# Product and GELU of two 16 MB tensors: 32 KB load rows, and the first stores from the scalar engine's queue

## The chip, the cores and the metric

One core of a Trainium2 chip. The metric is device time in microseconds of one launch; the median of 3 runs of the kernel before is 120.79 us (120.77 to 120.79). Engines named below: DVE is the vector engine, ACT the scalar engine, SP the sync engine, which here only issues transfers. Transfers (DMAs) are carried by 16 DMA engines, whoever issues them.

## The reference

```python
batch, dim = 1024, 4096          # x and y, float32
z = x * y
out = 0.5 * z * (1 + np.tanh(np.sqrt(2 / np.pi) * (z + 0.044715 * z ** 3)))
```

That is the tanh form of GELU on an elementwise product. Two tensors of 16.8 MB are read and one is written: 50.33 MB in all.

## The kernel before

Each tensor is viewed as 128 partitions of 32768 float32 columns, where a partition's columns lie in one piece in memory. "Columns a to b" below always means these, on all 128 partitions; 8192 columns are 4 MiB.

`xs` holds all 32768 columns of x in SBUF. The product and the GELU are written over it in place, and the stores read from it. `ys` is a ring of 16384 columns for y.

Loads are issued by SP (lines 64 to 78): x in two pieces of 16384 columns (x0, x1), y in one piece of 16384 (y0) and two of 8192 (y1, y2), which take the ring's first and second half again. x0 and y0 are moved by `_hoist` ahead of the start-up barrier. y1 and y2 each wait until two, or four, products are done (line 77), since they overwrite what these read.

The arithmetic goes in eight steps of 4096 columns (`STEP`). For each, DVE multiplies `xs` by `ys` into `xs` (line 87) and raises `sem_mul`; ACT waits for that and applies the GELU in place (line 94) and raises `sem_act`. DVE waits for a piece of y and the matching piece of x only at the start of that piece of y (lines 84 and 85).

Stores are issued by SP too (lines 98 to 100), after all loads: columns 0 to 16384 after four GELUs, and 16384 to 32768 after eight. SP then waits for both stores, clears the range of semaphores and ends. All transfers thus stand in one queue, in the order x0, y0, x1, y1, y2, store 0, store 1, and each of a transfer's 128 rows is one piece of 64 KB or 32 KB, eight rows to a DMA engine.

Of the kernel before, what the change touches and what calls it, by code (L numbers as in the profile page):

```python
# [1 line left out]

# [4 lines left out]


F32 = mybir.dt.float32
GELU = mybir.ActivationFunctionType.Gelu_apprx_tanh  # L10


X_LOADS = [(0, 16384), (16384, 32768)]

Y_LOADS = [(0, 16384, 0), (16384, 24576, 0), (24576, 32768, 8192)]
STEP = 4096
STORES = [(0, 16384), (16384, 32768)]
Y_RING = 16384


def _hoist(nc, issued):

    here = nc.cur_bb.bb.instructions
    first = nc.main_func.blocks[0].instructions
    for ins in issued:
        del here[next(k for k, i in enumerate(here) if i is ins or i.name == ins.name)]
    engine = issued[0].engine
    at = next(
        k
        for k, i in enumerate(first)  # L30
        if i.engine == engine and type(i).__name__ == "InstDrain"
    )
    first[at:at] = issued


@with_exitstack
def kernel(
    ctx: ExitStack,
    tc: tile.TileContext,
    x: bass.AP,  # L40
    y: bass.AP,
    out: bass.AP,
):
    nc = tc.nc
    P = nc.NUM_PARTITIONS

    x_r = x.flatten_outer_dims().rearrange("(p a) c -> p (a c)", p=P)
    y_r = y.flatten_outer_dims().rearrange("(p a) c -> p (a c)", p=P)
    out_r = out.flatten_outer_dims().rearrange("(p a) c -> p (a c)", p=P)
    total_f = x_r.shape[1]  # L50


    tc.close()
    tc.compile()  # L54

    xs = nc.alloc_sbuf_tensor("xs", [P, total_f], F32).ap()
    ys = nc.alloc_sbuf_tensor("ys", [P, Y_RING], F32).ap()
    sem_x = [nc.alloc_semaphore(f"sem_x{i}") for i in range(len(X_LOADS))]
    sem_y = [nc.alloc_semaphore(f"sem_y{i}") for i in range(len(Y_LOADS))]
    sem_o = [nc.alloc_semaphore(f"sem_o{i}") for i in range(len(STORES))]  # L60
    sem_mul = nc.alloc_semaphore("sem_mul")
    sem_act = nc.alloc_semaphore("sem_act")

    def load_x(i):
        a, b = X_LOADS[i]
        return nc.sync.dma_start(out=xs[:, a:b], in_=x_r[:, a:b]).then_inc(sem_x[i], 16)  # L66

    def load_y(i):
        a, b, r = Y_LOADS[i]
        return nc.sync.dma_start(  # L70
            out=ys[:, r : r + b - a], in_=y_r[:, a:b]
        ).then_inc(sem_y[i], 16)

    _hoist(nc, [load_x(0).ins, load_y(0).ins])
    load_x(1)
    for i in (1, 2):
        nc.sync.wait_ge(sem_mul, (Y_LOADS[i][1] - Y_LOADS[1][0]) // STEP)
        load_y(i)

    n = 0  # L80
    for i, (a, b, r) in enumerate(Y_LOADS):
        for j, (xa, xb) in enumerate(X_LOADS):
            if xa <= a < xb:
                nc.vector.wait_ge(sem_x[j], 16)
        nc.vector.wait_ge(sem_y[i], 16)  # L85
        for c in range(a, b, STEP):
            nc.vector.tensor_mul(  # L87
                out=xs[:, c : c + STEP],
                in0=xs[:, c : c + STEP],
                in1=ys[:, r + c - a : r + c - a + STEP],  # L90
            ).then_inc(sem_mul, 1)
            n += 1
            nc.scalar.wait_ge(sem_mul, n)
            nc.scalar.activation(  # L94
                out=xs[:, c : c + STEP], in_=xs[:, c : c + STEP], func=GELU
            ).then_inc(sem_act, 1)

    for i, (a, b) in enumerate(STORES):
        nc.sync.wait_ge(sem_act, b // STEP)
        nc.sync.dma_start(out=out_r[:, a:b], in_=xs[:, a:b]).then_inc(sem_o[i], 16)  # L100
    for i in range(len(STORES)):
        nc.sync.wait_ge(sem_o[i], 16)
    nums = sorted(s.num for s in [*sem_x, *sem_y, *sem_o, sem_mul, sem_act])
    assert nums == list(range(nums[0], nums[-1] + 1))
    nc.sync.sem_clear(range(nums[0], nums[-1] + 1))


# [1 line left out]
_INS = ['x', 'y']  # L109
_OUTS = [((1024, 4096), 'float32')]  # L110


# [23 lines left out]
```

## Time and profile before

| | us |
|---|---|
| median of the runs | 120.79 |
| the profiled execution | 120.85 |
| its span, first to last instruction | 119.5 |
| one product, DVE, 128 x 4096 (8 of them) | 4.42 |
| one GELU, ACT, 128 x 4096 (8 of them) | 3.62 |
| SP's issue of one DMA | 0.33 to 0.43 |
| SP waiting for products before y1 and y2 | 56.2 |
| SP waiting for GELUs before the stores | 33.8 |

The page gives each engine's busy time, a strip of 40 slices of the span with a digit for the busy share in each, and the queues' share of the 16 DMA engines' time. The chain lists what ended last, followed back to what released it. For DMAs the trace gives the time of issue on the queue of the engine that issues ("SPq") and the time from issue to landing, which includes waiting behind earlier transfers in the queue. L87 means line 87 of the kernel before.

### The profile page before, as it was taken

Reading aid. Unit: us, or ns where it says so; the run is one execution under the profiler, and the core shown is the slowest. Engines: PE = TensorE matmul, PEld = TensorE weight load, DVE = VectorE, ACT = ScalarE, POOL = GpSimd, SP = SyncE. Lnnn points to the kernel's source line nnn. Section 1 sums busy time; section 2 is a strip of 40 time slices with the busy share of each in tenths; the row PEclk is TensorE's granted clock in tenths of the full one; section 3 lists DMA queues with packets and bytes.
Section 4 is the critical chain, followed back from the end, with each engine's and each line's share of the span. In section 5 each row is a group of like instructions: output and inputs, shape, how many; then the busy total and the mean of one; then the engine's idle time right before and its main releaser. Section 6 shows DMA issues by size and latency. Waiting matters only on the chain.

```text
span 119.5 us, 68 instructions
## 1 busy us (share of the span) xinstructions
DVE 35.0 (29%) x8; ACT 30.2 (25%) x9; POOL 0.2 (0%) x4
## 2 busy tenths in 40 slices
DVE  0000000000000199999600049959990000000000
ACT  3000000000000006797780000977479200000000
POOL 0000000000000000000000000000000000000000
DMA  9889888998899889988898989998899888988890
GB/s 351 351 373 680 351 351 351 636 417 351 351 636 417 351 351 526 526 351 351 351 526 351 504 373 482 395 526 351 351 395 658 351 351 351 702 351 351 351 680 22
DMA packets 1008, 50.33 MB, mean 421 GB/s; under 512 B 112, under 2 KB 112, under 8 KB 112
## 3 DMA queue, kind: packets, MB, share of 16 engines
q1 hardware_dynamic: 1008, 50.33, 98.5%
HBM read 33.55 MB, written 16.78 MB: 421 GB/s over the span
## 4 chain that ended last, share of the span: by engine, by line
DMA 53%; DVE 22%; ACT 3%; SPq 0%; issue 0%; DVEq 0%
DMA ys<-in_y_dram 53%; DVE xs L87 22%; ACT xs L94 3%; SPq L66 0%; DVEq L85 0%
## 5 line engine op out<-in xcount | busy, mean ns | idle before, releaser
L87 DVE TENSOR_TENSOR xs<-xs,ys 128x4096 f32<-128x4096 f32 x8 | 35.0, 4421 | 54.7 <-DMA ys<-in_y_dram 54.7
L94 ACT ACTIVATE xs<-xs 128x4096 f32<-128x4096 f32 x8 | 28.9, 3617 | 61.1 <-DVE xs L87 61.1
L94 ACT ACT_TABLE_LOAD x1 | 1.3, 1283 | 1.9 <-PEq L54 1.9
L120 POOL MEMSET const-bfloat16-1.0<- 128x1 bf16 x1 | 0.1, 102 | 0.0
L120 POOL MEMSET const-uint8-127<- 128x1 uint8 x1 | 0.1, 102 | 0.0
L120 POOL MEMSET const-float32-1.0<- 128x1 f32 x1 | 0.1, 99 | 0.0
L120 POOL MEMSET const-float32-0.0<- 128x1 f32 x1 | 0.1, 98 | 0.2 <-issue 0.2
## 6 DMA issues: line engine op xcount, KB each, us to landing
ys<-in_y_dram SPq DMA_DIRECT2D x2, 4096.0 KB, 21.1
xs<-in_x_dram SPq DMA_DIRECT2D x2, 40.3
out_dram<-xs SPq DMA_DIRECT2D x2, 31.9
ys<-in_y_dram SPq DMA_DIRECT2D x1, 40.8
```

Source lines behind the costliest of these rows:

```text
L87: nc.vector.tensor_mul(out=xs[:, c : c + STEP], in0=xs[:, c : c + STEP], in1=ys[:, r + c - a : r + c - a + STEP],).then_inc(sem_mul, 1)
L94: nc.scalar.activation(out=xs[:, c : c + STEP], in_=xs[:, c : c + STEP], func=GELU).then_inc(sem_act, 1)
L120: nc = _bacc.Bacc("TRN2", target_bir_lowering=False, num_devices=1)
```

## The change

X and y are both loaded in four pieces of 8192 columns. SP's order of issue becomes x0, y0 (hoisted), x1, y1, x2, x3, then y2 after two products and y3 after four. Output is stored in four pieces: columns 0 to 4096 and 4096 to 8192 are issued by ACT, each right after the GELU that finishes it; 8192 to 24576 (after six GELUs) and 24576 to 32768 (after eight) are issued by SP behind the loads. Stores of 4096 columns have rows of 16 KB. SP no longer waits for the last store before it clears the semaphores: that store's semaphore is left out of the cleared range, waited for last, and lowered by 16 in the same instruction.

```diff
-X_LOADS = [(0, 16384), (16384, 32768)]
+X_LOADS = [(0, 8192), (8192, 16384), (16384, 24576), (24576, 32768)]
-Y_LOADS = [(0, 16384, 0), (16384, 24576, 0), (24576, 32768, 8192)]
+Y_LOADS = [(0, 8192, 0), (8192, 16384, 8192), (16384, 24576, 0), (24576, 32768, 8192)]
 STEP = 4096
-STORES = [(0, 16384), (16384, 32768)]
+STORES = [(0, 4096), (4096, 8192), (8192, 24576), (24576, 32768)]
+EARLY = 2
...
+    def store(engine, i):
+        a, b = STORES[i]
+        engine.wait_ge(sem_act, b // STEP)
+        engine.dma_start(out=out_r[:, a:b], in_=xs[:, a:b]).then_inc(sem_o[i], 16)
+
     _hoist(nc, [load_x(0).ins, load_y(0).ins])
     load_x(1)
-    for i in (1, 2):
-        nc.sync.wait_ge(sem_mul, (Y_LOADS[i][1] - Y_LOADS[1][0]) // STEP)
+    load_y(1)
+    load_x(2)
+    load_x(3)
+    for i in (2, 3):
+        nc.sync.wait_ge(sem_mul, (Y_LOADS[i][1] - Y_RING) // STEP)
         load_y(i)
...
             ).then_inc(sem_act, 1)
+            if n <= EARLY:
+                store(nc.scalar, n - 1)
 
-    for i, (a, b) in enumerate(STORES):
-        nc.sync.wait_ge(sem_act, b // STEP)
-        nc.sync.dma_start(out=out_r[:, a:b], in_=xs[:, a:b]).then_inc(sem_o[i], 16)
-    for i in range(len(STORES)):
+    for i in range(EARLY, len(STORES)):
+        store(nc.sync, i)
+    for i in range(len(STORES) - 1):
         nc.sync.wait_ge(sem_o[i], 16)
-    nums = sorted(s.num for s in [*sem_x, *sem_y, *sem_o, sem_mul, sem_act])
+    nums = sorted(s.num for s in [*sem_x, *sem_y, *sem_o[:-1], sem_mul, sem_act])
...
     nc.sync.sem_clear(range(nums[0], nums[-1] + 1))
+    nc.sync.wait_ge(sem_o[-1], 16).then_inc(sem_o[-1], -16)
```

More of the change, by code (lines that the diff above doesn't have):

```diff
@@ L59 @@
     sem_y = [nc.alloc_semaphore(f"sem_y{i}") for i in range(len(Y_LOADS))]
-    sem_o = [nc.alloc_semaphore(f"sem_o{i}") for i in range(len(STORES))]
     sem_mul = nc.alloc_semaphore("sem_mul")
     sem_act = nc.alloc_semaphore("sem_act")
+    sem_o = [nc.alloc_semaphore(f"sem_o{i}") for i in range(len(STORES))]
     def load_x(i):
```

## The prediction, made before the changed kernel was run

> **What bounds the kernel now.** I read the slices of the page first, then the DMA queue, the chain, the DMA issues with their times to landing, and last the start in narrow windows.
>
> ```profile
> span 119.5 us, 68 instructions
> DVE 35.0 (29%) x8; ACT 30.2 (25%) x9; POOL 0.2 (0%) x4
> ...
> DMA  9889888998899889988898989998899888988890
> ...
> q1 hardware_dynamic: 1008, 50.33, 98.5%
> ```
>
> The vector engine works 35 of 119.5 us and the scalar engine 30; the 16 DMA engines work all the time, on one queue. So the end is set by bytes divided by the rate, plus any moment in which the ring of transfers runs dry. There is none now. The chain in order of time shows what the arithmetic hides under:
>
> ```profile
> 0.44 40.80 DMA ys<-in_y_dram
> ...
> 41.34 17.43 DVE L87 TENSOR_TENSOR xs<-xs,ys 128x4096 f32<-128x4096 f32 x4 [41.34 <-DMA ys<-in_y_dram]
> 45.80 3.62 ACT L94 ACTIVATE xs<-xs 128x4096 f32<-128x4096 f32 x1 [42.59 <-DVE xs L87]
> ...
> 62.45 31.22 SPq L100 DMA_DIRECT2D out_dram<-xs  x2
> 70.47 8.76 DVE L87 TENSOR_TENSOR xs<-xs,ys 128x4096 f32<-128x4096 f32 x2 [11.70 <-DMA ys<-in_y_dram]
> ...
> 80.88 8.76 DVE L87 TENSOR_TENSOR xs<-xs,ys 128x4096 f32<-128x4096 f32 x2 [1.66 <-DMA ys<-in_y_dram]
> ```
>
> The first line is from the chain (start, length), the others from the timeline. The first store is issued at 62.45, when the loads still need until 80.8: it waits in the ring, and the rings go from loads to stores without a pause. The first store carries 19.3 us of work, and the second is issued at 93.3, before the first has ended. That order is what hides the last products and GELUs.
>
> Issue plus time to landing gives the landings. The spread of each line's issues is:
>
> ```profile
> L66 SPq DMA_DIRECT2D xs<-in_x_dram x2: 328/357/386, 0.0 to 1.9; - x2
> DMA to landing us min/median/max: 21.9/40.3/58.7
> ...
> L70 SPq DMA_DIRECT2D ys<-in_y_dram x3: 328/328/433, 0.4 to 58.8; - x3
> ...
> DMA to landing us min/median/max: 20.2/22.0/40.8
> ...
> L100 SPq DMA_DIRECT2D out_dram<-xs x2: 343/346/348, 62.4 to 93.3; - x2
> ...
> DMA to landing us min/median/max: 26.1/31.9/37.7
> ```
>
> Landings: y0 0.44+40.8 = 41.24; x1 1.93+58.7 = 60.6; y1 50.13+20.2 = 70.3; y2 58.80+22.0 = 80.8; store 0 62.4+37.7 = 100.1; store 1 93.3+26.1 = 119.4. Call 8192 columns (4 MiB) a unit. Differences: x1 19.4 for two units, y1 9.7 for one, y2 10.45 for one, store 1 19.3 for two. So a unit takes 9.67 us, loaded or stored, in 64 KB or in 32 KB rows, with one exception: the load just before the first store took about 0.75 more. The start costs 41.24 - 4 x 9.67 = 2.56. Of it 1.0 is from the issue to the first row:
>
> ```profile
> 0.00:1.00 1.00, 0.00 (x0) 0.00 (x0) 0.20 (x4) 1.00 0.00 0
> 1.00:2.00 1.00, 0.00 (x0) 0.07 (x1) 0.00 (x0) 1.00 3.13 1049
> ```
>
> (The last two columns are DMA share and GB/s, booked at the start of a row.) The other 1.56 is filling the pipeline and the receipt at the end.
>
> **What the Trainium skill says.** All from "DMA: Bandwidth & Descriptors". *Where 436 GB/s comes from*: a ceiling of 435.2 GB/s. The trace agrees: store 1, 8.39 MB in 19.3 us, is 435 GB/s; there is no faster rate to win while engines move one row at a time. *Queues, rings and completion order*: each DMA engine takes turns between queue rows that have work, a packet at a time. The kernel before has one queue, so nothing in its trace shows this. *Anatomy of one DMA*: DMA engines don't wait on semaphores; the issuing sequencer does, before dispatch. The trace agrees: store 0 was issued at 62.45, right after the fourth GELU (58.80+3.62). So a store whose GELU is late is not in the ring at all.
>
> **The change, part by part.** Times on the profiled execution's axis.
>
> *All loads in 32 KB rows.* The skill (same page, *Why small descriptors are slow*) prices a packet at about 3 cycles, 3.5 ns at its 850 MHz. Rows per engine go from 56 to 96 (eight for each of 7 transfers before; of 12 after), so 40 x 3.5 ns = 0.14 us as an estimate; the two row sizes measured above can't be told apart. I take 0.15. What moves is the first arithmetic: y0 with 8192 columns lands at 2.56 + 2 x 9.67 = 21.9 and not at 41.24. The vector engine starts at 22.0; two products (8.77) end at 30.8. SP issues four loads at 1.9 without waits, then y2 (waits for product 2, 30.8) and y3 (product 4). Ring order on SP: x0 y0 x1 y1 x2 x3 y2 y3, then the two late stores.
>
> *Early stores from the ACT queue.* GELU 1 runs 26.5 to 30.1 and ACT issues store 0 (about 0.35, from the SP issues). GELU 2 can start only at 30.8, when product 2 ends, so the issue and its wait on ACT's own GELU are covered; without that cover they would shift ACT by 0.35, which nobody awaits there. GELU 2 ends at 34.4, store 1 follows. From 31.1 on, each engine has 16 rows of 16 KB on the second ring, each 9.67/16 = 0.60 us. In turn with 32 KB load rows (1.21) they are through after 16 turns of 1.81, at about 60. They are bytes that had to be moved anyway, only earlier: the sum of bytes is unchanged. y1 lands at 2.56 + 38.7 + 4.8 = 46.1, product 4 ends at 54.9, y3 is issued then; x2, x3 and y2 lie before it in the ring until 80, so that wait is covered by 25 us.
>
> *What a change between load and store rows costs* is the unknown, 16 times. From above: the 0.75 before the first store now, 16 x 0.75 = 12 us. From below: nothing, if two rings are fetched ahead separately; and less than nothing if a store row and a load row overlap in an engine, at most all 9.67 us. I take 0.03 each, 0.5 in all, because 0.75 appears once per stage and looks like a refill that a second ring already has in hand.
>
> *The late stores.* Here is the cost that decides. Loads and early stores together are nine units: y2 (the eighth unit in effect) lands at 2.56 + 8 x 9.67 + 0.1 = 80.0, y3 at 89.7. After y3 the rings are empty unless a late store has been issued. Store 2 covers columns 8192 to 24576 and so waits for GELU 6, which needs y2: start 80.1, two products 8.77, to 88.9; GELU 3.62, to 92.5. First row 1.0 later, 93.5. So the DMA engines stand idle from 89.7 (89.3 without the receipt) to 93.5, about 4 us, where before they never did. Then the pipeline fills again: between 0.3 and 1.2 (load start above: 1.56 less a receipt of about 0.35); I take 0.8. Then three units, 29.0, and the receipt 0.35: 93.5 + 0.8 + 29.0 + 0.35 = 123.7. Store 3 must be ready before store 2 is through at 113: y3's products run 89.8 to 98.5, GELU 8 to 102.2. It is, with 11 us to spare. The 0.75 before the first store goes away in the gap; it isn't in this sum.
>
> *Short end.* The range clear is done before the last wait. From the last landing, 119.4, to the end of the span, 119.5, is 0.1: the gain is 0 to 0.1, I take 0.05.
>
> Sum: 123.7 + 0.1 - 0.05 = 123.75 without the cost of changes, 124.25 with it. Against the span of 119.5 that is +4.7. Outside the span the profiled execution had 120.85 - 119.5 = 1.35; it lies 0.06 above the median of 120.79, so the forecast is 120.79 + 4.7 = 125.5.
>
> **Rivals.**
> *Dear changes (slower still).* Each change of direction costs more than 0.2 us, up to the 0.75 seen. For it: y2's 10.45 against 9.7. Against it: seen once, in one ring. Everything after 31 moves later by 16 times the price, the gap stays: 125.0 + 3.2 to 12 = 128.2 to 137.
> *Overlap (faster).* In the mixed stretch of 31 to 60 us a store row's read of SBUF and write of HBM run beside a load row's opposite directions in the same engine. Price: up to 9.67 saved, which would give 125.0 - 9.67 = 115.3. It decides once more than 4.2 us, 43% of the early stores, is hidden. For it: load and store share neither side of the path. Against it: stages of pure loads and pure stores run at the same 435 GB/s, which speaks for a limit inside the engine that both share. Less than 43% gives 121 to 124.5.
> *The stores don't take turns.* If ACT's rows get through only when SP's ring is empty, they move at 79.9 to 89.6, fill the gap, and y2 lands 9.67 earlier; store 2 is then ready at 83. Nothing is idle, and the 0.75 stays: 120.79 + 0.15 - 0.05 = 120.9.
>
> **How the numbers follow.** My own case (changes at most 0.2 each, fill 0.3 to 1.2) gives 124.3 to 128.2: chance 0.60. Dear changes 0.17, about half of it under 131. Overlap past the threshold 0.13, below it 0.05. No turns 0.05. The range reaches from 120.6 (no turns) to 131, leaving out the overlap and the dear half of the changes, about 0.2. A measurement here tells 0.2% (0.24 us) from no change. Faster 0.14 (overlap, and a part of no turns); same 0.03 (no turns); slower 0.83.
>
> **What would show it.** Right: a second DMA queue moving from about 31 to 60; DMA share of zero between about 90 and 93.5, and the chain running y2, two products, GELU 6, store 2 to the end; SP waiting for ACT at line 78. The rate in 31 to 60 gives the price of a change: 435 GB/s is none, 400 about 0.15 each. Wrong: y2 landing well before 80 (overlap), the ACT queue moving after 70 (no turns), or no idle stretch after y3.

## The result, and the profile after

The changed kernel takes 125.1 us (median of 6 runs, 124.97 to 125.42), the kernel before in the same comparison 120.87. The ratio is 1.0348, 95% interval 1.0327 to 1.0369: slower by 3.5%. The forecast was 125.5. The profiled execution took 124.97, its span is 123.6.

The arithmetic is what it was; the page of the changed kernel shows the difference in the strip of the DMA engines (slices of 3.1 us) and in a second queue:

```profile
span 123.6 us, 75 instructions
...
DMA  9897989999979989989999997979707997793977
GB/s 329 350 509 339 509 371 477 392 456 466 376 307 466 498 350 424 498 355 429 429 488 445 403 509 339 509 339 509 339 0 339 572 445 339 339 678 170 509 339 339
...
q1 hardware_dynamic: 1440, 46.14, 87.6%
q10 hardware_dynamic: 288, 4.19, 7.9%
```

One slice moves nothing, the thirtieth: 89.6 to 92.7. Before, the one queue was busy for 98.5% of the span; now the two are for 95.5%. Narrow windows give the edges (as in the prediction, the last two columns are DMA share and GB/s):

```profile
88.00:89.00 1.00, 1.00 (x1) 0.75 (x1) 0.00 (x0) 1.00 1.21 524
89.00:90.00 1.00, 0.43 (x1) 0.54 (x1) 0.00 (x0) 1.00 0.01 0
90.00:91.00 1.00, 0.63 (x1) 1.00 (x1) 0.00 (x0) 1.00 0.00 0
91.00:92.00 1.00, 1.00 (x1) 1.00 (x1) 0.00 (x0) 1.00 0.00 0
92.00:93.00 1.00, 1.00 (x1) 1.00 (x1) 0.00 (x0) 1.00 0.00 0
93.00:94.00 1.00, 1.00 (x1) 0.08 (x1) 0.00 (x0) 1.00 1.07 459
```

A row's bytes are booked where it starts, so the stretch from 89 to 90, which shows nothing, still holds the ends of rows. By the records of single rows (the trace has the start, length, size and queue of each) the last row of y3 ends at 89.89 and the first row of store 2 starts at 93.95: 4.06 us idle. The timeline of the changed kernel (start, length, engine, line) names what they waited for:

```profile
80.67 8.76 DVE L96 TENSOR_TENSOR xs<-xs,ys 128x4096 f32<-128x4096 f32 x2 [25.95 <-DMA ys<-in_y_dram]
85.13 3.62 ACT L103 ACTIVATE xs<-xs 128x4096 f32<-128x4096 f32 x1 [26.76 <-DVE xs L96]
89.46 3.62 ACT L103 ACTIVATE xs<-xs 128x4096 f32<-128x4096 f32 x1 [0.72 <-DVE xs L96]
90.37 8.76 DVE L96 TENSOR_TENSOR xs<-xs,ys 128x4096 f32<-128x4096 f32 x2 [0.94 <-DMA ys<-in_y_dram]
93.11 10.05 SPq L78 DMA_DIRECT2D out_dram<-xs  x2
```

y2's products start at 80.67, GELU 6 ends at 93.08, SP issues store 2 at 93.11. The chain of waits doesn't show this: it follows the instruction that ended last, GELU 8 at 102.8, back through y3, and is silent on the transfers after it. No store is on it; SP's own waits do have the late one:

```profile
DMA ys<-in_y_dram 64%; DVE xs L96 14%; ACT xs L103 3%; SPq L67 0%; DVEq L94 0%
...
SPq L78 <- ACT xs L103: 47.4, 2, 38.0
```

Where DMA is the bound, as here, the windows find a hole and the timeline explains it.

### The profile page after: what moved, and what is told of

It is laid out like the page before. It is cut to its first block, busy times and chain, and to the rows that moved or that the text cites. A ratio compares the mean times of both kernels' runs of the same rounds, so it can differ in the third digit from the quotient of the medians.

```text
span 123.6 us, 75 instructions
## 1 busy us (share of the span) xinstructions
DVE 35.0 (28%) x8; ACT 30.2 (24%) x9; POOL 0.2 (0%) x4
## 4 chain that ended last, share of the span: by engine, by line
DMA 64%; DVE 14%; ACT 3%; SPq 0%; issue 0%; DVEq 0%
DMA ys<-in_y_dram 64%; DVE xs L96 14%; ACT xs L103 3%; SPq L67 0%; DVEq L94 0%
```

## The experiments

All edits are on the changed kernel unless said otherwise. Medians in us, ratios to the kernel before in the same comparison.

| run | median | ratio, 95% interval |
|---|---|---|
| e1_split_late_store | 120.81 | 0.9993 (0.9986 to 1.0) |
| e2_no_early_stores | 120.83 | 0.9993 (0.9983 to 1.0003) |
| e3_loads_alone | 120.96 | 1.0 (0.9991 to 1.001) |
| e4_early_8KB_rows | 124.46 | 1.0293 (1.028 to 1.0306) |
| e5_early_4KB_rows | 120.56 | 0.9967 (0.9955 to 0.9978) |
| e6_tiny_store_at_start | 120.96 | 1.0003 (0.9995 to 1.0011) |
| e7_tiny_store_at_30us | 120.89 | 0.9995 (0.9986 to 1.0004) |
| e8_late_wait_alone | 124.5 | 1.0297 (1.0282 to 1.0311) |
| e9_4KB_and_split | 120.95 | 1.0003 (0.9996 to 1.001) |
| e10_2KB_and_split | 122.61 | 1.0144 (1.0129 to 1.016) |
| e11_4KB_again | 120.57 | 0.9974 (0.9966 to 0.9981) |

The theory: a late store waits for a GELU that comes after the rings have run dry (the gap theory). The main rival: loads and stores in turn slow each other (the mixing theory).

**Take the wait away, keep the mixing.**

```diff
-STORES = [(0, 4096), (4096, 8192), (8192, 24576), (24576, 32768)]
+STORES = [(0, 4096), (4096, 8192), (8192, 16384), (16384, 24576), (24576, 32768)]
```

> Edit: the late store of columns 8192 to 24576 becomes two, 8192 to 16384 (needs GELU 4) and 16384 to 24576 (needs GELU 6). Gap theory: GELU 4 ends at about 58, so the first of them is in the ring long before y3 lands at 90, moves until about 99.5, and GELU 6 is done at 93; no idle stretch, about 4.1 us less than the changed kernel: 121.0, or 120.3 if the once-paid 0.7 us at the first store next to loads isn't paid again when loads go over to stores. Rival (mixing loads and stores is what costs): the mixed stretch is unchanged, so the time stays near 125.

Timeline of this kernel:

```profile
58.36 35.14 SPq L78 DMA_DIRECT2D out_dram<-xs  x2
80.72 8.76 DVE L96 TENSOR_TENSOR xs<-xs,ys 128x4096 f32<-128x4096 f32 x2 [26.04 <-DMA ys<-in_y_dram]
```

The first late store is issued at 58.36; y2's products start at 80.72, against 80.67 in the changed kernel. The mixed stretch is the same to 0.05 us, the rows leave no idle stretch once they have begun, and 120.81 is 4.3 below the changed kernel. All of the loss is gone.

**Take the mixing away, keep the wait.**

```diff
-STORES = [(0, 4096), (4096, 8192), (8192, 24576), (24576, 32768)]
-EARLY = 2
+STORES = [(0, 24576), (24576, 32768)]
+EARLY = 0
```

> Edit: no early store at all; two stores behind the loads, columns 0 to 24576 (needs GELU 6) and 24576 to 32768. Gap theory: y3 lands at about 80, GELU 6 ends at 82.9, first store row 83.7; idle about 4.0; then four units of 9.67: span 122.9 to 123.2, time 124.2 to 124.5 (the once-paid 0.7 falls into the gap). Mixing theory: nothing is mixed, so 120.8.

Windows and timeline of this kernel:

```profile
80.00:81.00 1.00, 0.79 (x1) 1.00 (x1) 0.00 (x0) 1.00 0.00 0
81.00:82.00 1.00, 1.00 (x1) 1.00 (x1) 0.00 (x0) 1.00 0.00 0
82.00:83.00 1.00, 1.00 (x1) 0.90 (x1) 0.00 (x0) 1.00 0.00 0
83.00:84.00 1.00, 1.00 (x1) 0.00 (x0) 0.00 (x0) 1.00 1.85 786
```

```profile
79.28 3.62 ACT L103 ACTIVATE xs<-xs 128x4096 f32<-128x4096 f32 x1 [0.72 <-DVE xs L96]
80.21 8.76 DVE L96 TENSOR_TENSOR xs<-xs,ys 128x4096 f32<-128x4096 f32 x2 [0.96 <-DMA ys<-in_y_dram]
82.93 10.07 SPq L78 DMA_DIRECT2D out_dram<-xs  x2
```

No store is early, nothing is mixed, and the same hole is there, ten microseconds sooner (rows 79.71 to 83.85: 4.14 us). The time is 124.5. With the two runs together the gap is the cause and the mixing isn't.

**The other parts of the change.** e2 has the change's loads and its short end, but two stores of 16384 columns behind the loads; e3 also has the old end.

```diff
-STORES = [(0, 4096), (4096, 8192), (8192, 24576), (24576, 32768)]
-EARLY = 2
+STORES = [(0, 16384), (16384, 32768)]
+EARLY = 0
```

> Edit: EARLY = 0 and the stores of the kernel before (two of 16384 columns, behind the loads, from SP); load rows and short end as changed. Gap theory: first store needs GELU 4 only, nothing idle; 120.6 to 120.9, as before. Mixing theory: the same. Theory that the load rows or the order x2, x3 ahead of y2 cost: above 121.5.

> Edit: only the 32 KB load rows and their order; stores and end as in the kernel before. The profile shows y0 and x0 in 0.2 us less than half of the time before, against 32 more rows per engine less 0 for stores at about 4 ns: 120.6 to 120.9. Less e2_no_early_stores, this is what the short end is worth: 0 to 0.1 us.

Both equal the kernel before within their intervals. (Two readings in the expectation of e3 are off: x0 and y0, landing at 21.7 where it was 41.2, took more than half of the time before, and the 0.2 us holds only against the predicted 21.9; and an engine has 24 more load rows, not 32.) The short end, 120.96 - 120.83 = 0.13, isn't resolved by intervals of 0.1% on each side.

**Are changes of direction free?** Smaller early rows mean more of them.

```diff
-STORES = [(0, 4096), (4096, 8192), (8192, 24576), (24576, 32768)]
-EARLY = 2
+STORES = [(0, 2048), (2048, 4096), (4096, 6144), (6144, 8192), (8192, 24576), (24576, 32768)]
+EARLY = 4
...
-        engine.wait_ge(sem_act, b // STEP)
+        engine.wait_ge(sem_act, -(-b // STEP))
```

(A store whose last column lies inside a step now waits for that step's GELU. Not shown: the loop in which ACT, after each GELU, issues all early stores that this GELU finishes. Runs e5 and e9 to e11 have both edits too, e7 the wait.)

> Edit: the early stores in four pieces of 2048 columns (rows of 8 KB), so 32 store rows per engine among the loads and not 16; the late stores as in the changed kernel. Gap theory with free changes of direction: 16 more rows at 4 ns, 125.1 to 125.4. If each change of direction costs 0.05 us (the 0.8 us missing in the mixed stretch, spread over 16 rows): 16 more of them, 125.9. If the 0.8 is paid once at the first store: no more than 125.4.

124.46: twice the changes of direction took 0.6 less, which neither theory had in its numbers. The trace shows why it fits the gap theory. The last row of y3 ends at the same time (89.88, against 89.89). But the 32 small store rows of each engine, one after each load row, reach to about 81, past the landing of y2, so fewer store bytes are moved ahead of y2. Its products start at 80.26 (80.67), store 2 is issued at 92.70 (93.11), and the hole is shorter by 0.4. So with 4 KB rows the hole should nearly close:

```diff
-STORES = [(0, 4096), (4096, 8192), (8192, 24576), (24576, 32768)]
-EARLY = 2
+STORES = [(k, k + 1024) for k in range(0, 8192, 1024)] + [(8192, 24576), (24576, 32768)]
+EARLY = 8
```

> Edit: early stores in eight pieces of 1024 columns (rows of 4 KB), late stores as in the changed kernel. Gap theory: y3 and the early stores still end at 89.9, but in turn with 40 load rows only 40 of the 64 store rows come before the end of y2; 24 rows of 0.15 us fewer stand before it, so y2 lands near 77.1, GELU 6 ends near 89.6, first late row 90.5: idle 0.6 instead of 4.1, total 121.3 to 121.9. Theory that the time is lost by mixing, or per change of direction: 48 changes more than the changed kernel has, so 125 or later.

The timeline and the windows of this kernel:

```profile
75.50 8.76 DVE L96 TENSOR_TENSOR xs<-xs,ys 128x4096 f32<-128x4096 f32 x2 [24.20 <-DMA ys<-in_y_dram]
...
86.43 8.76 DVE L96 TENSOR_TENSOR xs<-xs,ys 128x4096 f32<-128x4096 f32 x2 [2.17 <-DMA ys<-in_y_dram]
87.94 11.27 SPq L78 DMA_DIRECT2D out_dram<-xs  x2
```

```profile
86.00:87.00 1.00, 0.57 (x1) 1.00 (x1) 0.00 (x0) 1.00 1.04 426
87.00:88.00 1.00, 1.00 (x1) 0.92 (x1) 0.00 (x0) 1.00 1.02 418
88.00:89.00 1.00, 1.00 (x1) 0.00 (x0) 0.00 (x0) 1.00 1.03 422
```

y2's products start 5.2 us sooner than in the changed kernel (3.6 expected), y3 has landed by 86.4, and the early rows left over are moved alone at nearly the full rate until store 2 arrives. No hole, 120.56. The theory by change of direction (125 or later) falls. The 1.6 us by which y2 came sooner than expected are about what a miscount makes: the expectation put 40 store rows of each engine ahead of y2, and the records have 29 before y2's last row starts. The expectation let the early rows take turns with x1 too, but x1 lands at 31.6 and the first early row of most engines starts near 35. Eleven rows of 0.15 us are 1.65.

**Does 4 KB beat the kernel before, and does the split add to it?** e9 splits e5's late store at 16384; e10 does so with 2 KB rows; e11 is e5 once more.

```diff
-STORES = [(k, k + 1024) for k in range(0, 8192, 1024)] + [(8192, 24576), (24576, 32768)]
+STORES = [(k, k + 1024) for k in range(0, 8192, 1024)] + [(8192, 16384), (16384, 24576), (24576, 32768)]
```

> Edit: early stores in rows of 4 KB as in e5_early_4KB_rows, and the late store split at 16384 as in e1_split_late_store. e5 had no idle stretch left, so the gap theory gives the split nothing more: 120.4 to 120.7, the same as e5 within its spread. If e5's lead over the kernel before (0.33%) comes from small rows where loads and stores first meet (the 0.7 us cost less there), it stays; if it was scatter of few runs, 120.8 to 120.95.

> Edit: as e9_4KB_and_split with early rows of 2 KB (16 pieces of 512 columns). If smaller rows make the first meeting of loads and stores cheaper still: 0.2 to 0.4 below e9, about 120.2. If what small rows save is used up at 4 KB, or the 64 rows more at about 4 ns each (0.26 us) and 8 more issues on ACT count: 120.6 to 121.

> The kernel of e5_early_4KB_rows once more, in five rounds, because e9_4KB_and_split didn't keep its lead and its profiled execution shows transfers ending no earlier than before (119.04 against 119.07). If the lead is real, 120.5 to 120.6 against 120.9; if it was the scatter of eight runs on one chip, within 0.1% of the kernel before.

e11 repeats e5 (ratio 0.9974, 0.9966 to 0.9981): a gain of 0.26%, small but clear of no change, and the fastest form found. e9 loses it. The longest time to landing of an early store shows a difference:

```profile
DMA to landing us min/median/max: 15.5/42.1/82.7
```

That is e9; e5 has 15.1/41.4/53.4. With a late store already in SP's ring, the early rows never get the engines to themselves and go on in turn until the end, 36.9 + 82.7 = 119.6. Where exactly the 0.4 us are lost there is not shown. e10 fails in another way. Timeline of this kernel:

```profile
37.55 45.91 ACTq L78 DMA_DIRECT2D out_dram<-xs  x8
...
83.51 10.63 ACT L103 ACTIVATE xs<-xs 128x4096 f32<-128x4096 f32 x3 [45.99 <-issue]
```

The first eight issues on ACT took 0.37 to 0.50 us each; of the second eight, the first took 0.34, the next 11.2, and the last was not over before 83.5. ACT stood in its own issues for 46 us. GELU 3, whose product was done at 46.3, started at 83.51, and the first late store was issued at 90.66. The early rows left over kept the engines busy until 90.39; from there to 91.51 nothing moves, so 1.1 us of hole are back. The rest of the 2.0 us by which e10 is above e11 wasn't taken apart, nor what held ACT.

**The 0.7 us of the first store.** The prediction saw 0.75 us lost just before the first store of the kernel before. The two probes start from e2.

```diff
+    nc.vector.memset(warm, 0.0).then_inc(sem_w[0], 1)
+    nc.scalar.wait_ge(sem_w[0], 1)
+    nc.scalar.dma_start(out=out_r[:, 0:128], in_=warm).then_inc(sem_w[1], 16)
...
+    nc.sync.wait_ge(sem_w[1], 16)
     for i in range(EARLY, len(STORES)):
         store(nc.sync, i)
```

> Edit on the kernel without early stores: a small tile is filled by the vector engine and 128 columns of it (rows of 512 B) are stored from ACT at about 2 us, over columns that the proper store writes again later. Question: the 0.7 us which the first store costs the loads beside it. If it is a once-paid cost of the first store while the fill at the start hides it: gone at 80, total 120.1. If it is once paid but not hidden: y0 lands 0.7 later, total 120.8. If it belongs to going over from loads to stores in one queue: still there at 80, total 120.8 to 120.9 with y0 not later.

For e7:

```diff
-STORES = [(0, 16384), (16384, 32768)]
-EARLY = 0
+STORES = [(0, 128), (128, 16384), (16384, 32768)]
+EARLY = 1
```

> Edit on the kernel without early stores: ACT stores columns 0 to 128 (rows of 512 B) after GELU 1, at 30 us; the rest from SP behind the loads. If the first store costs 0.7 us once, whatever its size: products 3 and 4 start 0.7 later (41.9 and not 41.27), nothing at 80, total 120.8. If the cost goes with the bytes that a store has in flight: little at 30, 0.7 at 80, total 120.8 to 120.9. If a small first store pays for the large one: 120.2.

I compare the starts of the products of y2 and y3, one unit (9.67 us) apart if nothing is lost; first e2, then e8:

```profile
70.42 8.76 DVE L96 TENSOR_TENSOR xs<-xs,ys 128x4096 f32<-128x4096 f32 x2 [20.39 <-DMA ys<-in_y_dram]
80.87 8.76 DVE L96 TENSOR_TENSOR xs<-xs,ys 128x4096 f32<-128x4096 f32 x2 [1.69 <-DMA ys<-in_y_dram]
```

```profile
70.49 8.76 DVE L96 TENSOR_TENSOR xs<-xs,ys 128x4096 f32<-128x4096 f32 x2 [20.38 <-DMA ys<-in_y_dram]
```

In e2 they are 10.45 apart. e6: 70.62 and 81.09, 10.47. e7: 70.55 and 81.20, 10.65. A small store earlier doesn't pay for the large one. But e8, whose large store isn't in the ring yet, has 70.49 and 80.21, 9.72; and e1, in which stores had run in turn before, has 80.72 and 90.44, 9.72. So the loss comes where the first large store stands behind loads that still move, and e1 isn't charged for it again.

The records of single rows show where it sits. A 32 KB load row takes 1.213 us, but the last few rows of each engine before its first store row, and in some runs rows soon after it, take up to 2.1. What they take over 1.213, summed for one engine (mean of the 16):

| run | us from the start | excess, us |
|---|---|---|
| the kernel before | 76 to 80 | 0.70 |
| e2, e3, e6, e7 | 76 to 80 | 0.68, 0.50, 0.69, 0.81 |
| e8, no store in the ring yet | 76 to 80 | 0.00 |
| the changed kernel, 16 KB rows | 30 to 36 | 0.80 |
| e4, 8 KB rows | 30 to 42 | 0.55 |
| e5 and e11, 4 KB rows | 30 to 42 | 0.37 and 0.32 |

In the changed kernel no load row from 40 to 90 takes longer than 1.213: what mixing costs the load rows is paid where the first store meets them. With smaller store rows it is less there, and 0.70 less 0.32 to 0.37 is about the gain of e5 and e11 (0.4 and 0.3 us). That is an agreement of sizes, each from one trace, and not a test; e3 shows how far one trace can lie from the others. e9 (0.50) should then have kept 0.2 us and didn't (its trace is of the slowest of its 21 runs), and e10, with 0.08 at the first meeting, has another 0.39 from 76 to 82. What stretches the rows inside the DMA engines stays open.

## Why the prediction was right, point by point

- *The gap decides.* Shown by e1 and e8. Forecast: idle from 89.7 to 93.5; measured 89.89 to 93.95.
- *GELU 6 sets it.* Forecast end 92.5, without the 0.5 for changes of direction, which comes in only in the sum; measured 93.08. y2 was later by 0.6.
- *Price of changing direction.* Taken as 16 x 0.03 = 0.5. From the first product of y0 to that of y2, 21.78 to 80.67, is 58.9 for six units of 9.67, 58.0: 0.9 too much, and the long load rows before the first store row have 0.8 of it. e4 and e5 show that it doesn't grow with the number of changes. It is paid once and isn't a price per row, so the term had about the right size by luck. The rule for reading the rate fails with it. The window

```profile
31.00:60.00 29.00, 8.76 (x2) 10.43 (x3) 0.00 (x0) 1.00 0.98 410
```

would have meant over 0.1 for each of 16 changes, 1.6 or more in all.
- *Fill after the gap.* Taken as 0.8, between 0.3 and 1.2. Measured by single rows: an engine's first late row took up to 2.46 us, where a 64 KB row elsewhere takes 2.418, so at most 0.05. The range was drawn from the first load rows, which took about 0.6 us over the usual here as well; the first store rows after the hole didn't. Why isn't shown. This was the mis-sized term. The way from issue to first row was 0.84, not 1.0.
- *Start.* y0's products began at 21.78, forecast 22.0.
- *Sum.* Forecast span 124.25, measured 123.6: -0.2 from the start, +0.3 from the mixed stretch (0.9 against 0.5 and 0.1 for packets), -0.15 and -0.75 from issue and fill, and +0.25 because the three late units took 29.27 (93.95 to 123.22) and not 29.0 give 123.7. So the end came out within 0.6 us partly because errors of both signs, -1.1 and +0.55, met. The price of a row more was as taken, nearly nothing: a 64 KB row follows the one before after 2.414 us, a 32 KB row after 1.209, so about 4 ns each. The range given for the own case, 124.3 to 128.2, doesn't follow from its parts, which give 124.5 to 128.6; 125.1 lies in both.
- *In turn.* The Trainium skill ("DMA: Bandwidth & Descriptors", *Queues, rings and completion order*) has an engine take turns between its queues by the packet. Here the turn is a single row: while both queues have work, the records show one load row and one 16 KB store row in 1.82 us, the sum of 1.21 and 0.61. So the rival in which stores don't take turns is out, and so is overlap: the bytes are moved one after another, and early stores gain nothing. The turns were expected from 31 to 60; the first store row starts at 33.57, on most engines near 35, and the last ends at 62.05: after the issue at 29.89 an engine moved about four more load rows before its first store row.
- *Where it would show.* The idle stretch and SP's wait were as described. The chain was not: it ends at GELU 8 and has no store on it.

## What to carry to other kernels

In a kernel bound by transfers like this one, moving stores forward gains nothing by itself: it uses up work that would have covered the arithmetic at the turn from loads to stores. Count, at the moment the last load lands, what the queues still hold, and set it against the time until the next store's data are ready. Here, from the end of y2's rows, 12.4 us of products and GELU stood against 9.7 us of y3's rows, and 1.3 us more went to y2's landing and the start of the product (0.47) and to the issue and its way to the first row (0.87). That is the hole of 4.06. A store that spans ready and unready columns is as late as its last column, and cutting it at the boundary (e1) was worth 4.3 us.

## What the runs showed that I had not expected

- Smaller early rows were better, because rows taken in turn leave part of themselves for later: 8 KB rows shortened the gap by 0.4 us and 4 KB rows closed it.
- ACT, given 16 small stores to issue, was held in single issues for up to 11.2 us (e10), and a GELU behind them started 37 us after its product was ready. The same engine issued eight stores of twice the size in 0.34 to 0.48 us each (e5).
- The first large store behind moving loads costs about 0.7 us once (10.45 against 9.72 for a unit), in load rows that take up to 2.1 us in place of 1.213. A small store ahead of it doesn't take that away; smaller rows in the store itself make it less.
